# Raw gate weights in the ring of split operands, and eight single PSUM banks by turns, in the gate and up products of a two-layer encoder

## The chip, the cores and the metric

The kernel runs on one core of a Trainium2 chip. The metric is the device time of one execution in microseconds (us). Four compute engines work side by side, each through its own instructions in a fixed order: PE (matrix products), DVE (vector), ACT (scalar) and POOL (GpSimd). SP issues the DMA transfers, in order too. An instruction that waits holds up everything behind it on its engine or queue.

## The reference

Two layers, each a mixer of four head groups, then a gated MLP, then a gated embedding. The change lies in the MLP. With 1024 rows and 1024 columns of `h` and `D_FF` = 2816:

```
gate = dwconv_centred(h @ ffn_w_gate[i], ffn_conv_w[i], ffn_conv_b[i])
f = (jax.nn.silu(gate) * (h @ ffn_w_up[i])) @ ffn_w_down[i]
h = layer_norm(ALPHA * h + f, ln2_g[i], ln2_b[i])
```

`dwconv_centred` adds the three neighbouring rows of each column with three weights and a bias.

## The kernel before

**The stage.** `gate_up` makes `gate` and `up` for 22 features of 128 columns each (`NF`). A feature needs two 1024 x 128 blocks of weights, one of `ffn_w_up` and one of `ffn_w_gate`. Instead of eight half-size products it makes seven, from sums and differences of the halves of the weights and of the activations `B[...]`. One product is 12 matmuls of 128 x 512: four steps over the depth, and for each step three terms, since every fp32 operand is split into a rounded part and a remainder (`split`: ACT rounds, then DVE or POOL subtracts). The products of the first three features with `B["11"]` and `B["21"]` are made ahead of the loop (`starts`).

**One feature** (`feature`, line 1398): `load` (1370) issues the two transfers (line 1372) into the tag `wraw`, which has two buffers for both kinds. `s1` is the sum of the halves of the gate block and is DVE's first operation that needs the gate transfer; in the profile it is `s<-wraw`. From it come `w1`, `w2`, `w3`, `w4` and `w22`, the split operands, in the tag `H` with eight buffers (shared with the 1024-column rows of `h` that stages before and after hold there); DVE splits `w2` and `w3`, POOL the others, and POOL makes the differences `wraw<-s,wraw` and `wraw<-wraw`. After a product DVE adds its PSUM bank to a partial sum (`v`, `u`, `g`). I call these additions reads: they are what sets a bank free.

**PSUM.** `ps1` has four single banks (`ps` in the profile, `one`), `ps2` two tiles of two banks (`pp`, `two`). Products t2 and t1 of a feature share one two-bank tile `pa`, products t4 and 22 the other kind, `pb`; products 11, 12 and t3 take single banks.

**The gating of the feature before** (`gated`, 1432) stands in the middle of a feature: `conv3` is one ACT pass `g<-g,pp` and two DVE passes over 1023 columns (line 90), then ACT applies Silu, DVE multiplies the first half (`u<-u,g`) and POOL the second. `paired` (1444) sends the results to DRAM with SP (`put`, line 1446), for an even feature after one difference `k`, for an odd one after two sums and `k`.

**The order.** A scheduler lays out each engine's order from the program and gives out the buffers; nothing in the code fixes it line by line. All matmuls of products come from `mm` (line 99), DVE's and POOL's two-operand additions from line 87, ACT's from line 84. The stage runs from 818.5 to 1244.8 us in layer 0 and from 2395.1 to 2821.7 us in layer 1. After it `down` multiplies the stored features with `ffn_w_down` (matmuls at line 1613, its weights split into `part`).

Of the kernel before, what the change touches and what calls it, by code (L numbers as in the profile page):

```python
# [2 lines left out]

# [7 lines left out]
F32 = mybir.dt.float32  # L11
# [4 lines left out]
PSUM = bass.MemoryType.PSUM  # L16
# [58 lines left out]
class Trunk:  # L75
# [32 lines left out]

    def two(self):
        return self.ps2.tile([128, 1024], F32, name="pp", tag="pp")  # L110

    def load_w(self, src, shape, pool=None, tag="whl", eng=None, bufs=None):
        nc = self.nc
# [115 lines left out]
    def build(self):  # L229
        tc, ctx = self.tc, self.ctx  # L230
        self.ps1 = self.pool(ctx, "ps1", 4, space=PSUM)
        self.ps2 = self.pool(ctx, "ps2", 2, space=PSUM)
        self.dram = self.pool(ctx, "dram", 1, space=DRAM)
        self.sm = self.pool(ctx, "sm", 2)
        self.small_constants()
        self.wp = self.pool(ctx, "wp", 2)
        self.xp = self.pool(ctx, "xp", 8)
        self.khat = [[self.dram.tile([128, 3 if q == 0 else 2, 512], F32, name=f"khat{l}_{q}")
                      for q in range(8)] for l in range(L)]
        x = None  # L240
        for l in range(L):
            with ExitStack() as st:
                mu = self.pool(st, f"mu{l}")
                late = None
                if l == 0:
                    x, late = self.embed()
                else:
                    x, late = nxt
                rows = self.mixers(l, x, mu, late, st)
            hst = ExitStack()  # L250
            mid = self.out_proj(l, hst, *rows)
            nxt = self.rest(l, hst, *mid)
# [1102 lines left out]
    def gate_up(self, l, H, hp, x, fd):  # L1355
# [7 lines left out]
        with ExitStack() as st:  # L1363
            xq = self.pool(st, f"xq{l}", 6)
            fu = self.pool(st, f"fu{l}", 4)
            small = lambda: fu.tile([128, 512], F32, name="v", tag="v")
            big = lambda: fu.tile([128, T], F32, name="g", tag="g", bufs=2)
            B = {"11": x[0], "21": x[1]}

            def load(n, f):  # L1370
                w = self.wp.tile([128, 1024], F32, name="wraw", tag="wraw", bufs=2)
                nc.sync.dma_start(w.rearrange("p (k m) -> p k m", k=8), t[n][l, f])
                return w[:, 0:512], w[:, 512:1024]

            def part(src, pool, tag, eng=None):
                w = pool.tile([128, 2, 512], F32R, name="w2", tag=tag, **({"bufs": 4} if pool is self.wp else {}))
                self.split(w[:, 0], w[:, 1], src, eng or nc.gpsimd)
                return w

            def product(w, b, ps=None):  # L1380
                ps = self.one() if ps is None else ps
                wh, wl = [w[:, i].rearrange("p (k m) -> p k m", k=4) for i in range(2)]
                self.mm(ps, [z for k in range(4) for z in self.p3(wh[:, k], wl[:, k], b[0][:, k], b[1][:, k])])
                return ps

            def first(w1, w2, eng=None):

                v1, c11 = small(), fu.tile([128, 512], F32, name="u", tag="u", bufs=6)
                self.act(v1, product(part(w1, self.wp, "whl", eng), B["11"]))

                def second():
                    self.tt(c11, product(a12, B["21"]), v1, add)
                    return c11

                a12 = part(w2, self.wp, "whl", eng)
                return v1, second

            def feature(f, last, start=None):
                a11, a12 = load("ffn_w_up", f)
                a21, a22 = load("ffn_w_gate", f)  # L1400
                v1, c11 = start or first(a11, a12)
                s1 = fu.tile([128, 512], F32, name="s", tag="s", bufs=1)
                self.tt(s1, a21, a22, add)
                w1 = part(s1, hp, "H")
                self.tt(a21, a11, a21, sub)
                self.tt(a11, s1, a11, sub, nc.gpsimd)
                w2 = part(a11, hp, "H", nc.vector)
                w3 = part(a21, hp, "H", nc.vector)
                w22 = part(a22, hp, "H")
                self.tt(a12, a12, a11, sub, nc.gpsimd)  # L1410
                w4 = part(a12, hp, "H")
                lo, hi = slice(0, 512), slice(512, 1024)
                pa = self.two()
                u = small()
                self.tt(u, product(w2, B["t2"], pa[:, lo]), v1, add)
                u4 = small()
                self.tt(u4, product(w1, B["t1"], pa[:, hi]), u, add)
                if last:
                    gated(*last)
                g = big()  # L1420
                p7 = product(w3, B["t3"])
                self.tt(g[:, 512:1024], p7, u4, add)
                self.tt(u, p7, u, add)
                if start is None:
                    c11 = c11()
                pb = self.two()
                self.tt(g[:, 0:512], product(w22, B["t4"], pb[:, lo]), u, add)
                c12 = fu.tile([128, 512], F32, name="u", tag="u", bufs=6)
                self.tt(c12, product(w4, B["22"], pb[:, hi]), u4, add)
                return f, g, c11, c12  # L1430

            def gated(f, g, *cc):
                tg = big()
                self.conv3(tg, g, pp[:, C_FFC + 4 * f:C_FFC + 4 * f + 4])
                self.act(tg, tg, AF.Silu)
                for hf, c in enumerate(cc):
                    cs = slice(hf * 512, (hf + 1) * 512)
                    self.tt(c, c, tg[:, cs], ALU.mult, nc.gpsimd if hf else nc.vector)
                    if f >= PAIRED:
                        nc.sync.dma_start(fd[f][:, cs], c)  # L1440
                if f < PAIRED:
                    paired(f, *cc)

            def paired(f, c0, c1):

                put = lambda p, v: nc.sync.dma_start(fp[f // 4, p - 1][:, f // 2 % 2], v)
                spare = lambda: fu.tile([128, 512], F32, name="k", tag="k", bufs=1)
                if f % 2 == 0:
                    put(1, c0)
                    s3 = spare()  # L1450
                    self.tt(s3, c0, c1, sub)
                    put(7, s3)
                    kept[:] = c0, c1
                else:
                    a11, s1 = kept
                    put(2, c0)
                    put(4, c1)
                    self.tt(s1, s1, c1, add)
                    put(5, s1)
                    self.tt(a11, s1, a11, sub)  # L1460
                    put(6, a11)
                    s4 = spare()
                    self.tt(s4, c0, a11, sub)
                    put(3, s4)

            starts = []
            for f in range(3):
                v1, c11 = first(*load("ffn_w_up", f), nc.vector)
                starts.append((v1, c11()))
            for n in ("22", "t1", "t2", "t3", "t4"):  # L1470
                B[n] = [xq.tile([128, 4, 512], F32R, name="xq", tag="q") if n in ("t2", "t3", "t4") else
                        self.xp.tile([128, 4, 512], F32R, name="x", tag="X") for _ in range(2)]
            for j in range(4):
                h0, h1 = H[j], H[j + 4]
                a, b = slice(0, 512), slice(512, 1024)
                d = big()

                self.tt(h0[:, a], h1[:, a], h0[:, a], sub, nc.gpsimd)
                self.tt(d[:, b], h1[:, b], h1[:, a], sub, nc.gpsimd)
                self.tt(d[:, a], h1[:, b], h0[:, a], sub)  # L1480
                self.tt(h0[:, b], h0[:, b], d[:, a], sub, nc.gpsimd)
                p2 = self.two()
                self.blocks([(h1[:, b], p2[:, a], B["22"]), (h0[:, a], p2[:, b], B["t1"])], j)
                p2 = self.two()
                self.blocks([(d[:, b], p2[:, a], B["t3"]), (d[:, a], p2[:, b], B["t2"])], j)
                self.blocks([(h0[:, b], self.one(), B["t4"])], j)
            last = None
            for f in range(NF):
                last = feature(f, last, starts[f] if f < 3 else None)
            gated(*last)  # L1490

    def down(self, l, fd, hmid, H, end, ed):
        nc, t, pp = self.nc, self.t, self.pp[l]
# [341 lines left out]
```

## Time and profile before

| | us |
|---|---|
| median of 3 runs | 3201.98 (3198.91 to 3206.51) |
| the profiled execution | 3194.46 |
| its span, first to last instruction | 3192.7 |
| PE busy | 2946.4 (92%) |
| DVE busy | 2440.4 (76%) |
| POOL busy | 1771.2 (55%) |
| ACT busy | 1291.6 (40%) |

The mean granted clock of PE is 0.970 over the span. Busy time counts an engine as busy while it executes; the rest of the span it waits, either for a partner or for its own order. A row of the waits view names who was waited for, the total, how often, and the longest. In a timeline row the bracket at the end is the idle time just before and its releaser. The chain view follows the work that ended last back from the end.

### The profile page before, as it was taken

To read this page: it belongs to the slowest core of one execution; us is meant where nothing else is said; L and a number is where in the kernel's file an instruction comes from. 1 tells how busy PE (TensorE), PEld (TensorE's weight loads), DVE (VectorE), ACT (ScalarE), POOL (GpSimd) and SP (SyncE) were. 2 spreads that over 40 slices of the span, in tenths; PEclk is the share of its full clock that TensorE was granted. 3 is DMA by queue.
4 is the path that set the end of the run, shared out by engine and by line. 5 is a ranking of instruction groups with operands and counts; after the bars stand their busy time and mean duration, and the time that the engine had idled before them with its cause. 6 is when DMAs were issued, how large, how long until landed. Compare 5 with 4: busy or idle time off the path is not lost.

```text
span 3192.7 us, 40546 instructions
## 1 busy us (share of the span) xinstructions
PE 2946.4 (92%) x14316; PEld 2420.9 (76%) x14316; DVE 2440.4 (76%) x3711; ACT 1291.6 (40%) x2278; POOL 1771.2 (55%) x1371
## 2 busy tenths in 40 slices
PE   6999988999899999999989998889989999999996
PEld 4887866877678777787867877768767787777785
DVE  7678786878766777889777786868786677768986
ACT  4332365743333334443342333667333333344341
POOL 5455533527555666887435463335185556679845
PEclk9999998999999999999999998999999999999998
DMA  5466523022233326523335664130322333274332
GB/s 181 152 202 213 180 85 137 16 84 86 76 99 106 102 96 225 189 93 124 114 107 159 219 215 158 53 122 17 107 73 83 99 111 99 101 257 146 106 132 89
DMA packets 153427, 400.44 MB, mean 125 GB/s; under 512 B 16578, under 2 KB 43462, under 8 KB 152968
## 3 DMA queue, kind: packets, MB, share of 16 engines
q1 hardware_dynamic: 138968, 347.18, 32.5%
q0 software_dynamic: 14256, 50.67, 5.2%
q8 instruction: 114, 1.87, 0.2%
q14 instruction: 89, 0.73, 0.1%
HBM read 294.50 MB, written 103.28 MB: 125 GB/s over the span
## 4 chain that ended last, share of the span: by engine, by line
PE 48%; DVE 22%; POOL 9%; DMA 8%; issue 8%; ACT 5%; SPq 0%; DVEq 0%; POOLq 0%; ACTq 0%
PE ps L99 17%; PE pp L99 15%; PE ps L1613 7%; DMA wraw<-in_ffn_w_gate_dram 4%; POOL H L87 2%; DVE g L90 2%; DVE u L87 2%; PE ps L942 2%; DVE w L87 2%; POOL w L87 2%; DVE H L90 2%; PE ps L1054 1%; DVE v L87 1%; ACT w L84 1%; POOL wraw L87 1%
## 5 line engine op out<-in xcount | busy, mean ns | idle before, releaser
L99 PE MATMUL pp<-x,wh 128*128 128x512 f32 x1344 | 430.0, 398 | 1.8 <-ACT wh L84 1.8
L1613 PE MATMUL ps<-part 128*128 128x512 f32 x1440 | 341.4, 393 | 14.7 <-DVE H L87 6.1
L87 POOL TENSOR_TENSOR w<-wraw,w 128x512 fp32r<-128x512 f32 x164 | 232.7, 1431 | 206.0 <-ACT w L84 205.8
L1613 PEld LDWEIGHTS ps<-part 128*128 128x128 f32 x1440 | 270.8, 189 | 78.4 <-DVE H L87 9.8
L99 PEld LDWEIGHTS pp<-x,wh 128*128 128x128 f32 x1344 | 256.1, 193 | 54.2 <-ACT wh L84 2.0
L99 PE MATMUL ps<-x,w 128*128 128x512 f32 x1056 | 261.6, 395 | 10.8 <-ACT v L84 10.8
L99 PE MATMUL pp<-x,w 128*128 128x512 f32 x1056 | 258.3, 394 | 14.1 <-DVE v L87 9.7
L99 PE MATMUL pp<-x,wl 128*128 128x512 f32 x672 | 266.8, 397 | 3.8 <-POOL wl L87 3.8
L99 PE MATMUL pp<-xq,w 128*128 128x512 f32 x1056 | 264.4, 392 | 5.8 <-DVE x L87 4.5
L84 ACT ACTIVATE w<-wraw 128x512 fp32r<-128x512 f32 x264 | 152.8, 622 | 267.6 <-DMA wraw<-in_ffn_w_up_dram 169.9
L87 POOL TENSOR_TENSOR wl<-wraw,wh 128x1024 fp32r<-128x1024 f32 (+2 forms) x61 | 153.6, 2520 | 173.6 <-ACT wh L84 119.8
L99 PEld LDWEIGHTS pp<-x,w 128*128 128x128 f32 x1056 | 196.9, 188 | 63.7 <-DVE v L87 13.8
L87 POOL TENSOR_TENSOR part<-fr,part 128x512 fp32r<-128x512 f32 x140 | 220.5, 1602 | 43.7 <-ACT part L84 43.4
L99 PEld LDWEIGHTS ps<-x,w 128*128 128x128 f32 x1056 | 199.0, 190 | 59.9 <-ACT v L84 18.0
L99 PEld LDWEIGHTS pp<-xq,w 128*128 128x128 f32 x1056 | 198.0, 188 | 51.2 <-ACT w L84 5.1
L99 PE MATMUL ps<-wo,yn 128*128 128x512 f32 x768 | 188.0, 401 | 5.5 <-DVE H L90 3.1
L87 DVE TENSOR_TENSOR part<-wr,part 128x512 fp32r<-128x512 f32 x124 | 155.5, 1278 | 39.0 <-ACT part L84 38.7
L1039 POOL TENSOR_TENSOR P<-P,smr 128x1024 f32<-128x1024 f32 x64 | 121.2, 1895 | 110.1 <-DVE smr L1038 101.2
L99 PEld LDWEIGHTS ps<-wo,yn 128*128 128x128 f32 x768 | 145.4, 193 | 39.6 <-DVE H L90 5.4
L99 PE MATMUL ps<-wh,x 128*128 128x512 f32 x512 | 158.7, 390 | 0.0
L99 PEld LDWEIGHTS pp<-x,wl 128*128 128x128 f32 x672 | 129.1, 192 | 30.6 <-POOL wl L87 4.7
L90 DVE SCALAR_TENSOR_TENSOR g<-g,pp 128x1023 f32<-128x1023 f32 x88 | 128.4, 1460 | 27.0 <-ACT g L84 25.6
(385 smaller groups left out, 7264.5 us busy)
## 6 DMA issues: line engine op xcount, KB each, us to landing
fr<-fp SPq DMA_DIRECT2D x70, 512.0 KB, 3.7
c_fwd<-in_c_fwd_dram POOLq DMA_DIRECT2D x64, 512.0 KB, 5.4
wraw<-in_ffn_w_up_dram SPq DMA_DIRECT2D x50, 512.0 KB, 3.5
fp<-u SPq DMA_DIRECT2D x100, 256.0 KB, 2.4
wraw<-in_ffn_w_gate_dram SPq DMA_DIRECT2D x44, 512.0 KB, 3.8
wraw<-in_w_in_dram SPq DMA_DIRECT2D x42, 512.0 KB, 3.7
wr<-in_ffn_w_down_dram SPq DMA_DIRECT2D x36, 512.0 KB, 4.8
c_inv<-in_c_inv_dram POOLq DMA_DIRECT2D x32, 512.0 KB, 4.8
```

The source lines that it names most:

```text
L84: self.nc.scalar.activation(out, in_, func, **kw)
L87: (eng or self.nc.vector).tensor_tensor(out, a, b, op=op)
L90: return self.nc.vector.scalar_tensor_tensor(out, a, s, b, op0=op0, op1=op1)
L99: ins = self.nc.tensor.matmul(out, a, b, start=i == 0, stop=i == n - 1)
L942: ins = self.nc.tensor.matmul(out[0:64] if j else out, v[:, 0, :] if j else v.rearrange("p i d -> p (i d)"), terms[i][1 + j], start=k == 0 ...
L1039: nc.gpsimd.tensor_tensor(P, P, sm.to_broadcast([128, T]), op=ALU.mult)
L1054: nc.tensor.transpose(pt[:, j * 128:(j + 1) * 128], P[:, c0:c0 + 128], self.ident)
L1613: nc.tensor.matmul(ps, u, v, start=k == 0 and (p != 1 or ch == 0), stop=k == 5 and (p != 1 or ch == last))
```

## The change

The gate block is loaded into a buffer `wg` of the tag `H` (of its eight buffers a feature now takes six in turn, before it took five), and `wraw` keeps the up blocks alone. Around the loop over features the pool of two-bank tiles is closed (`swap2`) and reopened as four single banks `pt`; every product of the loop takes a bank from `pt` and from `ps` by turns. Afterwards the two-bank pool is opened again.

```diff
+    def swap2(self, name, bufs):
+        self.st2.close()
+        self.ps2 = self.st2.enter_context(self.tc.tile_pool(name=name, bufs=bufs, space=PSUM, reuse_waits="tile"))
...
-            def load(n, f):
-                w = self.wp.tile([128, 1024], F32, name="wraw", tag="wraw", bufs=2)
+            def load(n, f, pool=None):
+                w = hp.tile([128, 1024], F32, name="wg", tag="H") if pool else self.wp.tile([128, 1024], F32, name="wraw", tag="wraw", bufs=2)
...
-            def product(w, b, ps=None):
-                ps = self.one() if ps is None else ps
+            def product(w, b):
+                if next(turn):
+                    ps = self.ps2.tile([128, 512], F32, name="pt", tag="pt")
+                else:
+                    ps = self.one()
...
-                a21, a22 = load("ffn_w_gate", f)
+                a21, a22 = load("ffn_w_gate", f, hp)
...
-                pa = self.two()
...
-                self.tt(u, product(w2, B["t2"], pa[:, lo]), v1, add)
+                self.tt(u, product(w2, B["t2"]), v1, add)
...
-                self.tt(u4, product(w1, B["t1"], pa[:, hi]), u, add)
+                self.tt(u4, product(w1, B["t1"]), u, add)
...
-                pb = self.two()
-                self.tt(g[:, 0:512], product(w22, B["t4"], pb[:, lo]), u, add)
+                self.tt(g[:, 0:512], product(w22, B["t4"]), u, add)
...
-                self.tt(c12, product(w4, B["22"], pb[:, hi]), u4, add)
+                self.tt(c12, product(w4, B["22"]), u4, add)
...
+            turn = itertools.repeat(0)
...
+            turn = itertools.cycle((1, 0))
+            self.swap2(f"ps3_{l}", 4)
             for f in range(NF):
                 last = feature(f, last, starts[f] if f < 3 else None)
             gated(*last)
+            self.swap2(f"ps2_{l}", 2)
```

The scheduler's orders move with it. PE in the middle of layer 0's loop, where `w_` is a split operand with its number and `x`, `xq` are activations; before:

```order
L99 MATMUL ps<-x,w_9146 128x512 x3
L99 MATMUL pp<-x,w_9007 128x512 x12
L99 MATMUL ps<-x,w_9146 128x512 x9
L99 MATMUL ps<-x,w_9278 128x512 x12
L99 MATMUL pp<-xq,w_9156 128x512 x12
L99 MATMUL pp<-x,w_9022 128x512 x12
L99 MATMUL ps<-xq,w_9308 128x512 x12
```

and now:

```order
L100 MATMUL ps<-x,w_9007 128x512 x12
L100 MATMUL pt<-xq,w_9034 128x512 x12
L100 MATMUL ps<-x,w_9029 128x512 x12
L100 MATMUL pt<-xq,w_9037 128x512 x12
L100 MATMUL ps<-x,w_9024 128x512 x12
L100 MATMUL pt<-xq,w_9040 128x512 x12
L100 MATMUL ps<-x,w_9044 128x512 x12
```

The products of neighbouring features were interleaved, with one product cut by another; they now stand feature by feature, each in one piece, in the order of the program.

DVE in the last third of layer 0's loop, one odd feature's gating, from its `k` (the last difference sent to DRAM) to the product with Silu's result `g` of the next; before:

```order
L87 TENSOR_TENSOR k_10090<-u_9863,u_9714 128x512
L87 TENSOR_TENSOR u_10007<-ps_10109,v_10006 128x512
L87 TENSOR_TENSOR v_10063<-pp_10048,v_10049 128x512
L87 TENSOR_TENSOR g_10093<-ps_10094,v_10063 128x512
L87 TENSOR_TENSOR v_10049<-ps_10094,v_10049 128x512
L87 TENSOR_TENSOR s_10321<-wraw_10297 128x512
L87 TENSOR_TENSOR g_10093<-pp_10123,v_10049 128x512
L87 TENSOR_TENSOR wraw_10297<-wraw_10295,wraw_10297 128x512
L90 SCALAR_TENSOR_TENSOR g_10226<-g_10093,pp0_138,g_10226 128x1023 x2
L87 TENSOR_TENSOR w2_10328<-wraw_10295,w2_10328 128x512
L87 TENSOR_TENSOR v_10198<-pp_10197,v_10155 128x512
L87 TENSOR_TENSOR u_10007<-u_10007,g_10226 128x512
```

and now:

```order
L88 TENSOR_TENSOR k_10127<-u_9897,u_9746 128x512
L88 TENSOR_TENSOR g_10130<-ps_10131,v_10099 128x512
L88 TENSOR_TENSOR v_10084<-ps_10131,v_10084 128x512
L88 TENSOR_TENSOR s_10361<-wg_10337 128x512
L88 TENSOR_TENSOR u_10043<-pt_10146,v_10042 128x512
L88 TENSOR_TENSOR wg_10337<-wraw_10335,wg_10337 128x512
L88 TENSOR_TENSOR g_10130<-ps_10160,v_10084 128x512
L91 SCALAR_TENSOR_TENSOR g_10265<-g_10130,pp0_138,g_10265 128x1023
L88 TENSOR_TENSOR u_10174<-pt_10175,v_10099 128x512
L88 TENSOR_TENSOR w2_10368<-wraw_10335,w2_10368 128x512
L91 SCALAR_TENSOR_TENSOR g_10265<-g_10130,pp0_138,g_10265 128x1023
L88 TENSOR_TENSOR u_10043<-u_10043,g_10265 128x512
```

Between `k` and `s` there were four reads and now stand two (three after an even feature's `k`); between the second pass of the convolution and the product with Silu's result there were two operations and now there is none.

SP at the same place (names: `fp` is the DRAM copy of the features); before:

```order
L1446 DMA fp0_7499<-u_9844 128x512
L1372 DMA wraw_10295<-in_ffn_w_up_dram 128x1024
L1446 DMA fp0_7499<-u_9714 128x512
L1446 DMA fp0_7499<-k_10090 128x512
L1372 DMA wraw_10297<-in_ffn_w_gate_dram 128x1024
L1446 DMA fp0_7499<-u_10007 128x512
```

and now:

```order
L1453 DMA fp0_7499<-u_9877 128x512
L1453 DMA fp0_7499<-u_9746 128x512
L1453 DMA fp0_7499<-k_10127 128x512
L1379 DMA wg_10337<-in_ffn_w_gate_dram 128x1024
L1379 DMA wraw_10486<-in_ffn_w_up_dram 128x1024
L1453 DMA fp0_7499<-u_10043 128x512
```

The load of the gate block stands right behind the transfer of `k` in both; the load of the up block has moved from ahead of the last two transfers to behind the gate's.

## Rows read from the trace of the kernel before

**Rows 1.** The page, busy time of each engine over the span.
```profile
PE 2946.4 (92%) x14316; PEld 2420.9 (76%) x14316; DVE 2440.4 (76%) x3711; ACT 1291.6 (40%) x2278; POOL 1771.2 (55%) x1371
```
**Rows 2.** Stretches: from:to length, busy us (instructions) per engine, clock, DMA share, GB/s.
```profile
820.00:1240.00 420.00, 408.78 (x1763) 329.94 (x1762) 301.36 (x337) 141.35 (x209) 238.39 (x168) 1.00 0.33 110
1100.00:1220.00 120.00, 113.83 (x493) 91.61 (x492) 91.15 (x92) 39.37 (x58) 74.27 (x48) 1.00 0.28 93
```
**Rows 3.** Waits from 1100 to 1220 us: total us, times, longest us.
```profile
DVE s L87 <- DMA wraw<-in_ffn_w_gate_dram: 14.9, 6, 3.0
...
DVE g L90 <- ACT g L84: 6.5, 6, 1.4
...
PE pp L99 <- DVE v L87: 4.3, 3, 1.6
DVE k L87 <- POOL u L87: 4.2, 3, 1.4
DVE u L87 <- ACT g L84: 3.6, 3, 1.2
```
**Rows 4.** Waits of DVE in layer 1, 2600 to 2814 us.
```profile
DVE s L87 <- DMA wraw<-in_ffn_w_gate_dram: 22.2, 10, 3.1
```
**Rows 5.** Timeline (start, us, operation, idle before): DVE's first gate operation, features 0, 2, 5, 21.
```profile
790.81 3.00 POOL L87 TENSOR_TENSOR g<-H 128x512 f32<-128x512 f32 x2
...
790.89 1.76 DVE L87 TENSOR_TENSOR s<-wraw 128x512 f32<-128x512 f32 x1 [1.18 <-POOL H L87]
...
831.44 0.69 DVE L87 TENSOR_TENSOR s<-wraw 128x512 f32<-128x512 f32 x1 [5.34 <-DMA wraw<-in_ffn_w_gate_dram]
...
887.98 0.69 DVE L87 TENSOR_TENSOR s<-wraw 128x512 f32<-128x512 f32 x1 [3.97 <-DMA wraw<-in_ffn_w_gate_dram]
...
1203.28 0.69 DVE L87 TENSOR_TENSOR s<-wraw 128x512 f32<-128x512 f32 x1 [2.65 <-DMA wraw<-in_ffn_w_gate_dram]
```
**Rows 6.** The chain in order of time (start, us, what), two features.
```profile
1114.84 1.80 DVE k L87
1116.65 0.32 SPq L1446
...
1117.07 3.66 DMA wraw<-in_ffn_w_gate_dram
1120.76 0.70 DVE s L87
...
1136.67 0.70 DVE k L87
...
1137.80 5.07 DMA wraw<-in_ffn_w_gate_dram
1142.89 0.70 DVE s L87
```
**Rows 7.** Timeline of DVE around the convolution and Silu, in two features.
```profile
1104.50 3.71 DVE L90 SCALAR_TENSOR_TENSOR g<-g,pp 128x1023 f32<-128x1023 f32 x2 [0.78 <-ACT g L84]
...
1124.23 1.61 DVE L90 SCALAR_TENSOR_TENSOR g<-g,pp 128x1023 f32<-128x1023 f32 x1 [1.40 <-ACT g L84]
...
1129.92 0.69 DVE L87 TENSOR_TENSOR u<-u,g 128x512 f32<-128x512 f32 x1 [1.19 <-ACT g L84]
```
**Rows 8.** The chain, two products on PE without a wait.
```profile
1228.56 5.47 PE ps L99 x24
```
**Rows 9.** Operations on `wraw`, 1100 to 1220 us: ns min/median/max, first and last start.
```profile
L87 DVE TENSOR_TENSOR w<-wraw,w x12: 1452/1779/1796, 1108.1 to 1214.6; 128x512 fp32r<-128x512 f32 x12
L87 DVE TENSOR_TENSOR s<-wraw x6: 691/692/693, 1101.8 to 1203.3; 128x512 f32<-128x512 f32 x6
```
**Rows 10.** Timeline at the stage's end: DVE waiting for PE, then PE waiting in `down`.
```profile
1237.04 0.69 DVE L87 TENSOR_TENSOR v<-pp,v 128x512 f32<-128x512 f32 x1 [2.29 <-PE pp L99]
...
1246.07 3.37 PE L1613 MATMUL ps<-part 128*128 128x512 f32 x12 [1.08 <-ACT part L84]
...
1258.11 4.13 PE L1613 MATMUL ps<-part 128*128 128x512 f32 x10 [3.23 <-DVE H L90]
```

More of the change, by code (lines that the diff above doesn't have):

```diff
@@ L1 @@
+import itertools
 import math
@@ L231, in build @@
         self.ps1 = self.pool(ctx, "ps1", 4, space=PSUM)
-        self.ps2 = self.pool(ctx, "ps2", 2, space=PSUM)
+        self.st2 = ctx.enter_context(ExitStack())
+        self.ps2 = self.pool(self.st2, "ps2", 2, space=PSUM)
         self.dram = self.pool(ctx, "dram", 1, space=DRAM)
@@ L1411, in feature @@
                 w4 = part(a12, hp, "H")
-                lo, hi = slice(0, 512), slice(512, 1024)
-                pa = self.two()
                 u = small()
-                self.tt(u, product(w2, B["t2"], pa[:, lo]), v1, add)
+                self.tt(u, product(w2, B["t2"]), v1, add)
                 u4 = small()
-                self.tt(u4, product(w1, B["t1"], pa[:, hi]), u, add)
+                self.tt(u4, product(w1, B["t1"]), u, add)
                 if last:
```

## The prediction

> **What bounds the kernel now.** The page comes first: PE is busy 92% of the span, DVE 76% [rows 1]. By that PE is the bound, and a change that takes waits off PE should pay. The stage itself says something else, and four views show it.
>
> First the stretches. From 820 to 1240 us, layer 0's loop, PE carries 1763 matmuls [rows 2]. Without a wait 24 of them take 5.47 us [rows 8], 0.228 each, so 1763 need 401.8 and PE loses 18.2 of the 420 us. A feature of seven products, 84 matmuls, would take 84 x 0.228 = 19.15 us.
>
> Second, the pace. DVE's first gate operation comes at 887.98 for feature 5 and at 1203.28 for feature 21 [rows 5]: 315.3 us for 16 features, 19.71 each.
>
> Third, what DVE does in a feature. From 1100 to 1220 it is busy 91.15 us [rows 2] and waits 14.9 + 6.5 + 4.2 + 3.6 = 29.2 us [rows 3]: 120.35 of 120 us. So all its time is spent, and not one of these waits is for PE. Per feature that is 15.19 of work, 2.48 for the gate transfer, 1.08 for ACT's pass of the convolution, 0.60 for Silu and 0.70 for POOL's half of the gating: 20.05 us. **DVE in its own order is the bound, with its waits counted in**, and PE follows it. Layer 1 has the same wait for the gate transfer, ten times in ten [rows 4].
>
> Fourth, the chain shows where the gate wait comes from. `k` ends, SP sends `k`, only then does SP issue the gate transfer, and DVE's `s` waits for its landing: from 1116.64 to 1120.76 (4.12 us) and, behind more transfers, from 1137.37 to 1142.89 (5.52 us) [rows 6]. DVE is on both ends of that loop.
>
> **The change part by part.**
>
> *Single banks.* The two-bank tiles make t1 wait until t2's half is read; that shows as 4.3 us in three waits in 120 us [rows 3]. The change ends these waits. I value this at nothing: as long as DVE sets the pace, PE then waits for a bank eight products back, or for weights. It would be worth up to 18.2 us a layer if DVE were not the bound (first rival).
>
> *The gate block in the ring.* Its buffer now comes free earlier, which would let the load start earlier, but the order on SP still has it right behind the transfer of `k`, as before. So the 4.12 and 5.52 us stay. The up block's load moves behind it, where nobody waits for it soon: its operands are wanted about a feature later, and it would cost at most its own length, 3.7 us, in a feature where that cover is gone. It goes in at zero.
>
> *DVE's order.* Here is the cost. The wait for the gate is that loop less the reads that stand between `k` and `s`, about 0.69 us each (an operation of that size without a contest for the memory, [rows 9]). With four reads between, before, this makes 4.12 - 2.76 = 1.36 and 5.52 - 2.76 = 2.76, mean 2.06; the profile has 2.48, so the count is 0.4 short. With three reads after an even feature and two after an odd one, it makes 4.12 - 2.07 = 2.05 and 5.52 - 1.38 = 4.14, mean 3.09. I take 3.09.
>
> The pass of ACT in the convolution is waited for 0.78 us where something stood between and 1.40 where nothing did [rows 7]; the new order has every feature's last read right ahead of it, so 1.40. Silu is waited for 1.19 us where its product stands right behind the second pass [rows 7] and, in the other three of six features [rows 3], not at all, since two operations stand between; the new order has the first case each time, so 1.19. POOL's half, 0.70 on the average, is now read after at least two more operations: I take 0, at most 0.70. The work itself is unchanged, the same operations on the same sizes: 15.19.
>
> Sum of a feature: 15.19 + 3.09 + 1.40 + 1.19 = 20.87 us, against 19.71. Over the 16 features from 5 to 21: 16 x 1.16 = +18.6 us in each layer.
>
> Bounds: if the landing after an odd feature is as quick as after an even one, the gate wait is (2.05 + 2.74) / 2 = 2.40 and the sum 20.18, or +7.5; if POOL's 0.70 stays, it is 21.57, or +29.8.
>
> *The first features.* Two things differ. Feature 2's wait of 5.34 us for its gate transfer [rows 5] goes, since the loads of the first features find free buffers. On the other hand the load of feature 0 takes a buffer that POOL reads in the first of two operations at 790.81 (3.00 us for both), so until about 792.3; with a transfer of 3.66 [rows 6] `s` comes at 796.0 rather than 790.89 [rows 5], 5.1 later. Between -5.3 and +5.1 I take -3, nearer to the gain, because the work behind that late `s` (activations to be split and read) is partly done ahead of it in the new order.
>
> *The end.* Before, PE was the last at the end: DVE waited 2.29 us for it at 1237.04 [rows 10]. A DVE that comes late has that wait no more, -2.3. The rest of the lateness goes into `down`, whose first matmuls wait for weights that DVE splits (the 1.08 and 3.23 us of [rows 10] are such waits already).
>
> Sum: 18.6 - 3.0 - 2.3 = +13.3 us per layer, +26.6 in both; the bounds make it from 7.5 - 5.3 - 2.3 = -0.1 to 29.8 + 5.1 - 2.3 = +32.6 per layer. Layer 1's mixers have a slightly different order too, with the same operations; I take 0, and 5 us either way. The profiled execution took 3194.46 us, so it would become 3221.1. The median of the runs shown, 3201.98, is 7.5 above that execution, and the forecast goes on the median: **3228.6 us**.
>
> A sentence of the Trainium skill speaks for the change: Perfetto Trace Analysis, Matmul Optimizations, wants all eight PSUM banks in use, and its section Matmuls wants independent groups of matmuls to rotate through banks so that reading one overlaps the next. By that rule the lost 18.2 us a layer should mostly come back, which is the first rival. The trace agrees that the shared tile costs waits, but it puts 4.3 us of 120 on them.
>
> **The rivals.**
>
> *First: PE is set free* (faster). The waits at the banks go, features' operands lie ready one feature ahead, and PE runs through. Of 18.2 us some 2 remain in each layer, so 2 x 16 = 32 us are won: 3202 - 32 = 3170. For it: PE's busy share, and that PE can run without a wait [rows 8]. Against it: DVE's account, which has no slack. It needs a DVE feature of at most 19.15 us, which means a gate wait of at most 19.15 - 15.19 - 1.40 - 1.19 = 1.37 us instead of 3.09. That is the point from which it decides. Chance 0.15.
>
> *Second: nothing is seen.* The loads land sooner than in [rows 6] because the up block is no longer ahead of them, the gate wait is some 2.0 to 2.3 us, a feature takes 19.8 to 20.1, and the start pays for it: within 6 us, 3202. For it: the shorter of the two landings. Against it: the 5.52 us came with the transfer of `k` just ahead, which is there still. Chance 0.12.
>
> *Third: dearer still.* DVE's operations with both inputs in SBUF stretch beside POOL's: `w<-wraw,w` has a median of 1779 ns where `s<-wraw` has 692 [rows 9]. If the tighter order puts one more of them per feature beside a POOL operation, that is 1.09 us a feature, 17 us a layer more: 3229 + 35 = 3264. For it: Silu's product on DVE and POOL's half now become ready at the same moment. Against it: the number of such operations is the same and POOL is not busier. Chance 0.08.
>
> That the ring does not do what it is for is part of the forecast: the buffer is free, the load is not issued sooner.
>
> **How the numbers follow.** Forecast 0.65, from +8 to +45 us; rivals 0.15, 0.12 and 0.08. The predicted time is the forecast's, 3229. About 0.2%, 6.4 us, is what a measurement of this kernel can tell from no change. Faster by more than that is the first rival, 0.15; within it the second, 0.12; slower the forecast and the third, 0.73. The range leaves out the first rival and the dearer half of the third: from 3201, which takes in the greater part of the second and the low bound of the sum, to 3254, which is +26 a layer, short of the high bound.
>
> **What would show it.** The interval of `s<-wg` in the loop: 20.2 to 21.6 us if the forecast holds, 19.2 if PE is free. The wait of `s` for the gate transfer: near 3 us in each feature, or under 1.4. A wait of 1.2 us ahead of each `u<-u,g` and of 1.4 ahead of each first pass of the convolution. No waits for DVE at a half of a two-bank tile, but some at banks of eight products before. `down`'s first matmuls waiting for `part` by some 10 us more than the 1.08 and 3.23. The prediction is wrong in its main step if DVE is seen to wait for PE in the loop, or if the gate transfer is issued well before `k` ends.

## The result and the profile after

The changed kernel takes 3217.51 us (median of 5, 3214.34 to 3220.70) against 3201.98 (median of 5, 3197.83 to 3206.51): a ratio of 1.0054, 95% interval 1.0042 to 1.0067. It is slower by some 17 us, where 26.6 were forecast. Its profiled execution has a span of 3215.7 us against 3192.7.

The totals of PE and ACT hardly tell the two kernels apart. Those of DVE and POOL do: for the same number of operations DVE is busy 32.7 us longer and POOL 69.4. The page of the kernel after, to set beside [rows 1]:

```profile
PE 2965.1 (92%) x14316; PEld 2436.8 (76%) x14316; DVE 2473.1 (77%) x3711; ACT 1289.1 (40%) x2278; POOL 1840.6 (57%) x1371
```

The stretches (columns as in [rows 2]): in the same 420 us PE does 1752 matmuls instead of 1763, and in the second stretch DVE is still short of full by its busy time alone:

```profile
820.00:1240.00 420.00, 406.66 (x1752) 328.25 (x1752) 310.48 (x333) 138.75 (x207) 264.31 (x163) 0.99 0.29 98
1100.00:1220.00 120.00, 114.30 (x492) 91.32 (x491) 88.22 (x93) 39.27 (x59) 77.59 (x48) 1.00 0.27 96
```

The waits of DVE in the second stretch (total, times, longest), to set beside [rows 3]:

```profile
DVE s L88 <- DMA wg<-in_ffn_w_gate_dram: 14.4, 5, 3.2
DVE g L91 <- ACT g L85: 7.9, 6, 1.3
DVE u L88 <- ACT g L85: 7.1, 6, 1.2
```

Work and waits make 88.22 + 29.4 = 117.6 of 120 us; the sixth wait for the gate, which ends at 1220.55, would add what is missing. So DVE's time is spent in full after the change too, and the wait for PE is missing from its list, as before. The waits of PE on DVE's half of a two-bank tile are gone; in their place PE waits for weights that ACT rounds and for banks, in the same stretch:

```profile
PE pt L100 <- ACT w L85: 3.0, 3, 1.0
PE pt L100 <- DVE v L88: 2.2, 3, 0.9
```

DVE's timeline through one feature of layer 0 (start, us, operation, idle before) shows each of the three waits:

```profile
995.74 0.69 DVE L88 TENSOR_TENSOR s<-wg 128x512 f32<-128x512 f32 x1 [3.17 <-DMA wg<-in_ffn_w_gate_dram]
...
999.55 1.80 DVE L91 SCALAR_TENSOR_TENSOR g<-g,pp 128x1023 f32<-128x1023 f32 x1 [1.31 <-ACT g L85]
...
1002.98 2.31 DVE L91 SCALAR_TENSOR_TENSOR g<-g,pp 128x1023 f32<-128x1023 f32 x1
1006.48 0.69 DVE L88 TENSOR_TENSOR u<-u,g 128x512 f32<-128x512 f32 x1 [1.19 <-ACT g L85]
...
1015.05 0.69 DVE L88 TENSOR_TENSOR s<-wg 128x512 f32<-128x512 f32 x1 [2.48 <-DMA wg<-in_ffn_w_gate_dram]
```

and the chain ahead of the first of them is the loop of [rows 6], with `k`, its transfer, the gate's transfer and `s`:

```profile
990.27 1.11 DVE k L88
...
991.40 0.32 SPq L1453
...
991.81 3.91 DMA wg<-in_ffn_w_gate_dram
```

**Where the time went.** The second stretch holds the last features alone. Over 16 features of layer 0, from `s` of feature 5 to `s` of feature 21, before and after (the third busy time is DVE's):

```profile
887.98:1203.28 315.30, 307.08 (x1327) 247.77 (x1326) 228.02 (x259) 107.50 (x160) 180.16 (x128) 1.00 0.31 101
891.73:1220.55 328.82, 316.65 (x1364) 254.43 (x1363) 241.32 (x257) 106.44 (x160) 207.76 (x128) 1.00 0.28 96
```

DVE's idle time is 315.30 - 228.02 = 87.28 us before and 328.82 - 241.32 = 87.50 after: the same. What grew is its work, by 13.30 of the 13.52 us. In layer 1 it is 13.0 of 15.7 us (228.29 busy of 315.37, then 241.29 of 331.10). The two passes of the convolution are what got longer, by 19.7 us; all else on DVE got shorter by 6.4:

```profile
L90 DVE SCALAR_TENSOR_TENSOR g<-g,pp 128x1023 f32<-128x1023 f32 x32 | 46.1, 1441 | 7.7 <-ACT g L84 7.3
L91 DVE SCALAR_TENSOR_TENSOR g<-g,pp 128x1023 f32<-128x1023 f32 x32 | 65.8, 2057 | 21.0 <-ACT g L85 21.0
```

The timelines of DVE and POOL show what stands beside them. Before, both passes in 2.59 us, while POOL idles for 5.41 us up to 977.81:

```profile
973.46 2.59 DVE L90 SCALAR_TENSOR_TENSOR g<-g,pp 128x1023 f32<-128x1023 f32 x2
977.81 1.30 POOL L87 TENSOR_TENSOR w<-wraw,w 128x512 fp32r<-128x512 f32 x1 [5.41 <-ACT w L84]
```

After, beside the passes at 999.55 (1.80 us) and 1002.98 (2.31 us) shown above:

```profile
1000.23 2.28 POOL L88 TENSOR_TENSOR wraw<-wraw 128x512 f32<-128x512 f32 x1
1002.46 1.74 POOL L88 TENSOR_TENSOR w<-wraw,w 128x512 fp32r<-128x512 f32 x1
```

In those 16 features 19 of the 32 passes before have no POOL operation beside them, and each takes 1.27 to 1.29 us; after, none is without one, and each takes 1.80 to 2.31. That POOL's operation is the reason is read from these lengths; no run took it away.

### The profile page after: what moved, and what is told of

Its sections match the earlier page's. It is cut to its first block, busy times and chain, and to the rows that moved or that the text cites. A ratio compares the mean times of both kernels' runs of the same rounds, so it can differ in the third digit from the quotient of the medians.

```text
span 3215.7 us, 40648 instructions
## 1 busy us (share of the span) xinstructions
PE 2965.1 (92%) x14316; PEld 2436.8 (76%) x14316; DVE 2473.1 (77%) x3711; ACT 1289.1 (40%) x2278; POOL 1840.6 (57%) x1371
## 4 chain that ended last, share of the span: by engine, by line
PE 50%; DVE 22%; DMA 9%; issue 7%; POOL 7%; ACT 5%; SPq 1%; POOLq 0%; DVEq 0%; ACTq 0%
PE ps L100 18%; PE pp L100 12%; PE ps L1624 7%; PE pt L100 5%; DMA wg<-in_ffn_w_gate_dram 4%; DVE u L88 2%; POOL H L88 2%; DVE v L88 2%; PE ps L949 2%; DVE H L91 1%; ACT g L85 1%; DVE g L91 1%; DVE w L88 1%; PE ps L1519 1%; PE ps L1061 1%
## 5 line engine op out<-in xcount | busy, mean ns | idle before, releaser
L100 PE MATMUL ps<-x,w 128*128 128x512 f32 x1176 | 286.7, 394 | 6.1 <-ACT v L85 6.1
L100 PE MATMUL pt<-xq,w 128*128 128x512 f32 x840 | 207.5, 397 | 24.9 <-ACT w L85 15.7
L100 PE MATMUL pt<-x,w 128*128 128x512 f32 x936 | 226.3, 391 | 0.0
L91 DVE SCALAR_TENSOR_TENSOR g<-g,pp 128x1023 f32<-128x1023 f32 x88 | 170.2, 1934 | 51.9 <-ACT g L85 51.9
L100 PEld LDWEIGHTS pt<-xq,w 128*128 128x128 f32 x840 | 156.6, 189 | 68.9 <-ACT w L85 33.2
L88 POOL TENSOR_TENSOR w<-wraw,w 128x512 fp32r<-128x512 f32 x120 | 188.3, 1581 | 32.2 <-ACT w L85 32.2
L100 PEld LDWEIGHTS pt<-x,w 128*128 128x128 f32 x936 | 175.9, 188 | 38.0
L100 PE MATMUL ps<-xq,w 128*128 128x512 f32 x744 | 182.7, 395 | 2.8 <-ACT w L85 2.8
L100 PEld LDWEIGHTS ps<-xq,w 128*128 128x128 f32 x744 | 139.3, 189 | 38.6 <-ACT w L85 9.3
L85 ACT ACTIVATE w<-wraw 128x512 fp32r<-128x512 f32 x176 | 105.2, 622 | 136.0 <-POOL w L88 95.3
```

What stands on the lines that cost most here:

```text
L85: self.nc.scalar.activation(out, in_, func, **kw)
L88: (eng or self.nc.vector).tensor_tensor(out, a, b, op=op)
L91: return self.nc.vector.scalar_tensor_tensor(out, a, s, b, op0=op0, op1=op1)
L100: ins = self.nc.tensor.matmul(out, a, b, start=i == 0, stop=i == n - 1)
```

## The experiments

Theory 1: DVE's own order, waits counted in, sets the pace of the stage, and it waits for a gate load that SP issues only behind the transfer of DVE's `k`. Rivals: the ring costs the time; or the contest for the memory; or PE is the bound and the loss lies at the ends of the stage. All runs were timed in five rounds beside the kernel before, whose median was 3198.5 in the first four and 3198.7 in the last three.

**The single banks alone** (the gate block back in `wraw`):

```diff
-                a21, a22 = load("ffn_w_gate", f, hp)
+                a21, a22 = load("ffn_w_gate", f)
```

> The changed kernel with the gate block back in the two-buffer tag of the up block; the single banks by turns stay. Theory 1 (DVE's own order with its waits sets the pace, and the new order has fewer operations between k and the wait for the gate transfer): the single banks bring that order, so this is slower than the kernel before by 10 to 40 us, 3212 to 3242. Rival (the ring of split operands costs the time, because the gate block takes a buffer there and the first loads come late): the banks alone are no slower than before, 3175 to 3205.

Measured: 3245.56 us, ratio 1.0146 (1.0131 to 1.0162), +47 us, above the upper end of what theory 1 expected and on its side, though its reason, fewer operations between `k` and the wait, fits only the last features of the kernel before (see the gate term below). Its DVE waits from 900 to 1100 us:

```profile
DVE s L88 <- DMA wraw<-in_ffn_w_gate_dram: 31.6, 9, 4.1
DVE g L91 <- ACT g L85: 12.4, 9, 1.4
DVE u L88 <- ACT g L85: 11.9, 10, 1.2
DVE u L88 <- POOL u L88: 3.0, 5, 0.6
DVE k L88 <- POOL u L88: 3.0, 5, 0.6
```

3.5 us for the gate, 1.4 and 1.2 in the convolution, and a wait for POOL that the changed kernel does not have. The loss comes with the order that the single banks bring, and here it does lie in the waits. Over the same 16 features as above DVE works 231.43 us (228.02 before) and idles 109.37 (87.28):

```profile
890.19:1230.99 340.80, 319.84 (x1362) 254.03 (x1361) 231.43 (x257) 108.33 (x160) 199.05 (x129) 0.99 0.28 94
```

The passes of the convolution do not stretch: 1421 ns in the mean from 900 to 1100 us, 1344 before, 2070 in the changed kernel.

**The ring alone** (the kernel before, only its gate block in the tag `H`):

```diff
-            def load(n, f):
-                w = self.wp.tile([128, 1024], F32, name="wraw", tag="wraw", bufs=2)
+            def load(n, f, pool=None):
+                w = hp.tile([128, 1024], F32, name="wg", tag="H") if pool else self.wp.tile([128, 1024], F32, name="wraw", tag="wraw", bufs=2)
...
-                a21, a22 = load("ffn_w_gate", f)
+                a21, a22 = load("ffn_w_gate", f, hp)
```

> The kernel before with the gate block in the ring of split operands and the two-bank tiles kept. Theory 1: DVE's order between k and the gate operation stays about that of before and the gate load is still behind the transfer of k, so the time is that of before within 8 us, 3194 to 3210. Rival: the ring costs the time, 3212 or more.

Measured: 3192.02 us, ratio 0.9982 (0.9969 to 0.9996). It is 6 us faster, 2 us under the band of theory 1, and the rival that the ring is the cost falls for the ring alone. Its trace is not that of before, though. The 16 features take 306.48 us, 19.16 each, which is PE's own 19.15, and from 900 to 1100 us DVE waits 5.4 us for PE; but feature 5 starts 9.3 us later (897.27 against 887.98). The passes of the convolution stretch here too, to 1922 ns in the mean. So the stretching comes with the ring, while DVE's other operations take less:

```profile
897.27:1203.75 306.48, 300.60 (x1307) 245.83 (x1306) 218.73 (x256) 108.42 (x158) 201.69 (x128) 0.99 0.30 102
```

With the single banks the ring gives back most of their loss: +1.46% alone, +0.54% with the ring. It takes away the idle time that they bring (109.37 to 87.50 us in layer 0) and adds to DVE's work (231.43 to 241.32).

**The changed kernel, with the gate loads issued by ACT:**

```diff
-                nc.sync.dma_start(w.rearrange("p (k m) -> p k m", k=8), t[n][l, f])
+                (nc.scalar if pool else nc.sync).dma_start(w.rearrange("p (k m) -> p k m", k=8), t[n][l, f])
```

> The changed kernel with the gate loads issued by ACT instead of SP, so that none stands behind the transfer of k. Theory 1: the gate is there when DVE comes to it, a feature on DVE falls from some 20.5 to 17.8 to 18.6 us, below PE's 19.15, and PE is the bound: 3165 to 3190, faster than the kernel before. Rival: the loss comes from the ring or from the contest of DVE and POOL for the memory, the queue changes nothing: 3210 to 3225.

Measured: 3162.66 us, ratio 0.9885 (0.9868 to 0.9902): 36 us faster than before, and by the ratios 54 us faster than the change as it was made, by the queue alone. From 900 to 1100 us PE has no gap (200.00 us of 200, 878 matmuls, 0.228 each), while DVE does more in the same time than in the changed kernel (160.80 us, where that has 146.15):

```profile
900.00:1100.00 200.00, 200.00 (x878) 164.53 (x877) 160.80 (x175) 74.42 (x109) 138.29 (x88) 1.00 0.32 107
```

Its DVE waits in that stretch:

```profile
DVE g L91 <- ACT g L85: 14.5, 11, 1.3
DVE u L88 <- ACT g L85: 13.0, 11, 1.2
DVE s L88 <- DMA wg<-in_ffn_w_gate_dram: 7.4, 6, 1.7
DVE g L88 <- PE pt L100: 1.7, 1, 1.7
DVE u L88 <- PE pt L100: 1.4, 1, 1.4
```

The two waits of the convolution and of Silu stand as they were, 1.3 and 1.2 us a feature; only the wait for the gate has gone down, from about 3 us in each feature to 7.4 us over eleven features. And here DVE waits for PE, as with the ring alone and not in the changed kernel. In this kernel the passes of the convolution are as long as in the changed one (1968 ns in the mean): with PE as the bound they no longer cost anything that shows. The timeline of the two queues shows the load issued by ACT 2.9 us ahead of the transfer of `k` instead of 0.4 behind it:

```profile
969.79 0.33 ACTq L1379 DMA_DIRECT2D wg<-in_ffn_w_gate_dram  x1
972.72 0.32 SPq L1453 DMA_DIRECT2D fp<-k  x1
973.13 0.58 SPq L1379 DMA_DIRECT2D wraw<-in_ffn_w_up_dram  x1
```

**The kernel before, with the gate loads issued by ACT** (the same line, for `n == "ffn_w_gate"`):

> The kernel before with the gate loads issued by ACT. Theory 1: the gate's buffer comes free only when POOL has split the up or the gate block of the feature before, so the load starts hardly earlier: 0 to 12 us less than before, 3190 to 3202. Rival (the queue alone is the cost): as fast as the changed kernel with the same edit, 3165 to 3185.

Measured: 3196.09 us, ratio 0.9998 (0.9987 to 1.0010): nothing. The wait for the gate from 900 to 1100 us is still 24.3 us in nine times (29.9 in ten before). With two buffers for both kinds of blocks the load goes hardly earlier, whoever issues it: in one feature POOL's last split from the buffer ends at 967.13, ACT issues the load at 967.16, and SP sends `k` at 967.70. From 940 to 1010 us the lead is 0.3 to 2 us. Over the 16 features of layer 0 the wait for the gate does fall, from 48.8 us to 38.4, but DVE's work grows from 228.02 to 239.75; the run doesn't show why the two nearly balance. So the buffer and the queue have to be freed together: the ring alone gives -0.18%, the queue alone nothing, and both without the single banks -0.9% (the last run but one).

**The changed kernel, with DVE's first gate operation done twice:**

```diff
                 self.tt(s1, a21, a22, add)
+                self.tt(s1, a21, a22, add)
```

> The changed kernel with DVE's first gate operation (the sum of the two halves, 0.69 us) done twice in each of the 44 features. Theory 1 (DVE's order is the bound): the second one lies right behind the wait for the gate transfer and nothing hides it, 44 x 0.69 = 30 us at most, some less in the first features of a layer: 3237 to 3248. Rival (PE, or the memory ring, sets the pace): DVE is busy 77% of the span and takes it up, 3214 to 3222.

Measured: 3242.88 us, ratio 1.0147 (1.0130 to 1.0164), 25 us above the changed kernel as the two medians stand (0.93% by the ratios, 30 us). In the trace the 16 features of layer 0 take 339.35 us instead of 328.82, 0.66 more in each. One operation of 0.69 us in each of 44 features is on the path nearly in full, on an engine that is busy 77% of the span. That is theory 1's plainest sign.

**The ring and the ACT queue, with the two-bank tiles kept** (the edits of the second and the third run in the kernel before):

> The kernel before with the gate block in the ring and the gate loads issued by ACT, but the two-bank tiles kept: the faster version without the single banks. If the single banks are worth something once DVE no longer sets the pace, this is slower than that version (3162.7) by 8 to 30 us: 3170 to 3192. If the banks are worth nothing at any time, it is as fast, 3157 to 3168.

Measured: 3171.58 us, ratio 0.9910 (0.9896 to 0.9925), against 0.9885 (0.9868 to 0.9902) with single banks; by the medians 9 us slower, at the low end of what was expected if banks are worth something. The two intervals overlap a little, so this is a likely gain, not a proven one. The trace shows where it could come from: from 900 to 1100 us DVE waits 6.3 us for PE, PE once 0.9 us for DVE's read of a tile's first half, and PE makes 868 matmuls, ten fewer than with single banks:

```profile
900.00:1100.00 200.00, 198.97 (x868) 162.46 (x867) 170.41 (x171) 70.95 (x105) 147.18 (x86) 1.00 0.30 105
```

**The changed kernel, with the gated halves sent by ACT and the loads left on SP:**

```diff
-                put = lambda p, v: nc.sync.dma_start(fp[f // 4, p - 1][:, f // 2 % 2], v)
+                put = lambda p, v: nc.scalar.dma_start(fp[f // 4, p - 1][:, f // 2 % 2], v)
```

> The changed kernel with the gate loads on SP as they are, but the transfers of k and of the other gated halves issued by ACT, so that the gate load stands behind none of them. Theory 1 (what costs is the place behind k, not the queue that issues the load): as fast as with the gate loads on ACT, 3152 to 3175. Rival (loads issued by ACT land sooner, or SP is short of time): 3195 to 3220.

Measured: 3152.50 us, ratio 0.9856 (0.9841 to 0.9870), 46 us faster than before and the fastest kernel of this study. The loads are issued by SP as before; only what they stood behind is gone. So it is the place behind `k` and the other stores that costs, not the queue that issues. This run by itself could also mean that SP was short of time, since it takes work off SP. The changed kernel's trace speaks against it: from 900 to 1100 us SP waits 184 of the 200 us, 153.6 of them ahead of a store for DVE's `u`. Its stretch is as full as that of the third run:

```profile
900.00:1100.00 200.00, 200.00 (x878) 164.60 (x877) 162.26 (x174) 74.23 (x108) 139.81 (x88) 1.00 0.33 108
```

## Why the prediction was right, and where its working was off

**What bounds the kernel** was read right: DVE's account is full before and after, and one more operation on it shows in the time in full, although PE is the busiest engine on the page. The sign, the bound and the length of a feature came out. The source of the loss did not: the prediction put it into waits and the work at unchanged, and it was the work that grew.

**The feature on DVE**, forecast 20.87 us, measured in layer 0 from feature 5 to feature 21:

```profile
891.73 0.69 DVE L88 TENSOR_TENSOR s<-wg 128x512 f32<-128x512 f32 x1 [2.07 <-DMA wg<-in_ffn_w_gate_dram]
```

and

```profile
1220.55 0.69 DVE L88 TENSOR_TENSOR s<-wg 128x512 f32<-128x512 f32 x1 [2.45 <-DMA wg<-in_ffn_w_gate_dram]
```

328.82 / 16 = 20.55, and 331.10 / 16 = 20.69 in layer 1 (2475.42 to 2806.52), against 19.71 in both before. So the 16 features cost +13.5 and +15.7 us, where the sum had +18.6. Its parts, in the waits from 900 to 1100 us of the changed kernel:

```profile
DVE s L88 <- DMA wg<-in_ffn_w_gate_dram: 29.5, 10, 3.6
DVE u L88 <- ACT g L85: 11.9, 10, 1.2
DVE g L91 <- ACT g L85: 11.8, 9, 1.3
```

2.95 for the gate (forecast 3.09), 1.31 for the convolution (1.40), 1.19 for Silu (1.19), none for POOL (0). DVE's work is 146.15 us in 200, or 15.0 in a feature of 20.55 (15.19). Each part is near its forecast, but as a step up from the kernel before the forecast does not hold. Its account of before was read from 1100 to 1220 us, the last six features: 15.19 of work and 4.86 of waits, 20.05 in all, where the 16 features have 228.02 / 16 = 14.25 of work and 5.46 of waits, 19.71 in all. So the sum set 20.87, built on the one, against 19.71 of the other; its own terms differ by 20.87 - 20.05 = 0.82, where 0.84 was measured in layer 0. The agreement of these two is luck: the 0.82 were to be waits with the work unchanged, and the 0.84 are 0.83 of work and 0.01 of idle time.

The gate term shows why. Its step from 2.48 to 3.09 rests on four reads between `k` and `s` before. In layer 0 this holds, with three or four, for the last six features only; in the eleven ahead of them (5 to 15) there is none: `s` stands right behind `k`, in one feature even ahead of it:

```profile
982.96 0.69 DVE L87 TENSOR_TENSOR k<-u 128x512 f32<-128x512 f32 x1
986.76 0.69 DVE L87 TENSOR_TENSOR s<-wraw 128x512 f32<-128x512 f32 x1 [3.12 <-DMA wraw<-in_ffn_w_gate_dram]
```

The new order, with its two and three, puts more cover there on the whole, not less. From feature 6 to 21 the waits for the gate are 44.8 us before and 46.3 after, 0.1 more a feature, not 0.61 (0.4 in layer 1). Those of the convolution and of Silu grow, from 7.3 and 13.6 us to 21.0 and 19.0, but DVE's waits for POOL (13.4 us) and for ACT's rounding of `w` (4.9) go.

Within the gate term the two kinds of features came out nearer each other than forecast: about 3.2 after an odd feature and 2.4 after an even one (the two rows of `s<-wg` in the timeline above), where 4.14 and 2.05 were forecast. From the end of `k` at 991.38 to `s` at 995.74 are 4.36 us, not the 5.52 of [rows 6]: behind an odd feature the gate transfer took 3.91 us, not 5.07. The up block's load no longer stands ahead of it; that this is why it lands sooner is argued from the order on SP, no run shows it by itself.

**The first features**, forecast -3 from feature 0 to 5 against before, late start counted in. The profiled execution of the changed kernel was already 6.65 us late before the change can act: POOL's subtraction of [rows 5] starts at 797.46 instead of 790.81, after the same instructions. `s` of feature 0 comes 4.95 us after it, where before it came with it (forecast 5.1 later), and feature 5 comes 89.32 us later than feature 0, where before it took 97.09: -7.8 + 4.9 = -2.9.

```profile
797.46 2.52 POOL L88 TENSOR_TENSOR g<-H 128x512 f32<-128x512 f32 x2
...
802.41 1.85 DVE L88 TENSOR_TENSOR s<-wg 128x512 f32<-128x512 f32 x1 [4.86 <-DMA wg<-in_ffn_w_gate_dram]
```

**The end**, forecast to take 2.3 us back and to give the rest to `down`. PE's timeline there, to set beside [rows 10]:

```profile
1260.11 5.87 PE L1624 MATMUL ps<-part 128*128 128x512 f32 x16 [2.62 <-ACT part L85]
1270.33 3.78 PE L1624 MATMUL ps<-part 128*128 128x512 f32 x8 [4.34 <-DVE part L88]
1274.28 24.00 PE L1624 MATMUL ps<-part 128*128 128x512 f32 x102 [0.18 <-DVE H L91]
```

Feature 21 is 10.6 us late on DVE (1220.55 - 6.65 against 1203.28), and the long run of 102 matmuls in `down` starts at 1274.28 against 1258.11, 9.5 us late by the same measure. So 1.1 came back instead of 2.3, and the loss of the stage is paid in `down`, as the prediction had it: PE's last product of the stage ends at 1247.8 against 1245.0, some 4 us earlier than before when the 6.65 are taken off. In layer 1 the run starts at 2860.04 against 2835.92, 24.1 us late in all, 8.0 more than layer 0 left it. 9.5 + 8.0 = 17.5 us for both layers, and the medians say 15.5, the ratio 17.3. The forecast of 26.6 was half as much again. Most of it is the 0.2 to 0.3 us by which a feature was put too long (8.0 us in both layers); in layer 1 the stretch up to feature 5 also gave back more, 5.1 us where 3 were forecast.

**The rivals.** PE set free: the third and the last experiment show it happening at about the place where the prediction put its condition, a gate wait under 1.37 us (7.4 and 10.3 us from 900 to 1100, 0.7 and 1.0 in a feature), with -36 and -46 us, where 32 were worked out. That nothing is seen did not come. The third, dearer still, was given 0.08, and its time did not come, but its mechanism is the one that the changed kernel shows: DVE operations with both inputs in SBUF stretch beside POOL's. It was priced at 1.09 us a feature on top of the waits, and the passes of the convolution got 19.7 / 16 = 1.23 us longer. But the waits hardly grew in sum, and so the time stayed below even the forecast.

**The ring's purpose.** The prediction said that the buffer comes free and the load is not issued sooner. The third, the fourth and the last run show both halves: without the buffer, leaving the place behind `k` is worth nothing, and with the buffer it is worth 54 to 63 us by the ratios. With the ring alone the wait for the gate falls all the same, from 48.8 to 36.2 us in the 16 features of layer 0: the load still stands behind `k`, but more of DVE's operations stand ahead of `s` than in most features before.

The Trainium skill (Perfetto Trace Analysis, Matmuls) wants independent groups of matmuls to rotate through different PSUM banks. Single banks by turns came out the other way as long as DVE's order was the bound: +1.46% alone. For loops the Trainium skill (Perfetto Trace Analysis, DMA Optimizations) says that it may make sense to give inputs to one engine that can issue transfers and outputs to another. By that the last experiment was the thing to do, and the run agrees, with 0.9856.

## What to carry to other kernels

Add up an engine's work and its waits for others: an engine that is 75% busy but never waits for the busiest one can be the bound, and an edit that changes its order changes the time, by its waits and by what its operations then run beside. Do the sum over the whole loop, before and after, with work and waits apart: here the last six features stood for 16, and the loss was put into waits where the work had grown. A load that stands on a queue behind a store waits for whoever makes what is stored; a buffer that comes free early is worth little until the load can leave that place, and leaving it is worth nothing without the buffer.

## What was not expected of the hardware

That ACT can send the gated halves at no cost that shows: seven transfers for two features stand in its order, each behind the engine that makes its data, and PE still ran without a gap in that stretch. And that the single banks alone would cost as much as 47 us. In their trace a feature's wait for the gate is 3.5 us instead of the changed kernel's 2.95, and DVE waits for POOL's half, 6.0 us in 200, where the changed kernel never does; why both come back when the gate block shares the two buffers of `wraw` was not taken apart. Nor was it forecast that with the ring every pass of the convolution would run beside a POOL operation, and take 1.80 to 2.31 us in the changed kernel, where most took 1.27 to 1.29 before.
